# A two-layer hybrid block on one core: the second token tile's closing-norm steps and the next low parts queued behind the first tile's norm, two transfers issued from GpSimd's queue, and the last rows of the down weights split apart

## The chip, the cores and the metric

The kernel runs on one core of a Trainium2 chip. The metric is the device time of one execution in microseconds, the median of the runs; lower is better. The engines are named as the profile names them: PE (TensorE matmuls), PEld (its weight loads), DVE (VectorE), ACT (ScalarE), POOL (GpSimd) and SP (SyncE, which only issues transfers here). A name with a q (ACTq, SPq, POOLq) is that engine's instruction queue while it issues or waits.

## What is computed

Two layers act on 256 tokens of 1024 channels, all in float32. Each layer has a first feed-forward block, a mixer (convolution, recurrence and pooling side by side), cross-attention to a memory of 256 rows, and a second feed-forward block. Each of the four parts is closed by a layer norm of the residual sum. The change touches the feed-forward blocks and the norms that close them:

```python
def swiglu(x, w_gate, w_up, w_down):
    return (jax.nn.silu(x @ w_gate) * (x @ w_up)) @ w_down
...
for l in range(DEPTH):
    h = layer_norm(ALPHA * h + 0.5 * swiglu(h, ffn1_gate[l], ffn1_up[l], ffn1_down[l]), ln_g[l, 0], ln_b[l, 0])
    ...
    h = layer_norm(ALPHA * h + 0.5 * swiglu(h, ffn2_gate[l], ffn2_up[l], ffn2_down[l]), ln_g[l, 3], ln_b[l, 3])
return h
```

The line left out holds the mixer and the cross-attention, each with a layer norm of its own. The hidden width of the feed-forward blocks is 2816: five chunks of 512 columns and a last one of 256.

## The kernel before, in words

**Numbers in two parts.** PE multiplies a rounded form of float32. So every operand is split (`split`, L74 to L76): ACT casts it to the rounded form, the high part (`whi`, `ah`, `xTh`), and DVE subtracts that from the original and leaves the low part (`wlo`, `al`, `xTl`). A product is three matmuls into one sum: high by high, high by low, low by high (`mm_rows`, L153). Every weight passes through this: `load` (L78) issues the transfers of a slab of weights from SP into buffers called `raw` (six of 128 x 1024), and splits each buffer into a `whi` and a `wlo` (eight of each). A `raw` buffer is free for the next transfer once DVE has made its low part.

**Token tiles.** The 256 tokens are two tiles of 128, kept as `h[0]` and `h[1]` (`h0`, `h1` in the rows below). PE needs each of them transposed before the next block (`transposed`, L201: eight PE transposes, L196, whose results ACT and DVE split into `xT`).

**A feed-forward block** (`ffn`, L420) goes through the chunks. For each it makes the gate and up products, silu and their product, moves the result across partitions by four transfers (`turn`, L464, into a tile called `dealt`) and DVE transposes (L477), splits it into `ah` and `al`, and multiplies it by rows of the down weights into four sums `dn` (two tiles by two halves of the columns). In three of the four blocks the last chunk, 256 wide, goes through `by_seven` (L609): seven products of blocks in place of eight. There the gated product is made in the tile `both` (L723), two of its four transfers are issued by SP and two by ACT (L468, L469), and `slab(4, 0)`, `slab(4, 1)` and `slab(5, 0)` (L759) bring the last down weights. The products with these three slabs stand in the closing norm's function, by `tail` and `ending` (L846 to L862): all of tile 0 first, then tile 1's first half, then a part of its second half, then the transposes of `h[0]`, and the rest of tile 1.

**The closing norm** (`finish`, L323) does for tile 0 and then for tile 1: the residual sum of each half with its row sums (L352), the mean (L362), the sum of squares (L365, on ACT), the variance (L366), one over its root (L370, on POOL), subtraction of the mean and the gain (L373, two halves), scale and shift (L378, two halves). In the last norm of the program the statistics are made another way (L358, L368), and tile 1's second half is closed by two quarters (L339, L346).

**What sets the order.** Every engine runs its own instructions strictly in the order of its queue. That order is made by a scheduler when the program is built. `tc.issue_after(x)` is a hint to it: an instruction in that block which runs on the same engine as `x` is queued behind `x`. It puts nothing on the chip but the order. The norm of the first feed-forward block of layer 1 is followed by `keys` (L868), columns of `ca_k` by the memory `mT`; the norm of layer 0's second block is followed by the gate and up products of layer 1's first block (`first`, L494, the branch with `pend`), in which the transposes of `h[1]` (`pend`) stand in the middle of tile 0's up products.

Of the kernel before, what the change touches and what calls it, by code (L numbers as in the profile page):

```python
# [60 lines left out]
def model(ctx: ExitStack, tc: tile.TileContext, t: dict, out: bass.AP):  # L61
# [9 lines left out]

    loads, normed, lows, turns = [], [], [], []

    def split(hi, lo, src):  # L74
        nc.scalar.copy(hi, src)  # L75
        lows.append(nc.vector.tensor_tensor(lo, src, hi.bitcast(F32), op=ALU.subtract))  # L76

    def load(src, k0, nk, c0, ncol, fine=False, dealt=False, across=False):  # L78


        hi, lo, todo = [], [], []
        step = 2048 // ncol
        for a in range(k0, k0 + nk, step):
            half = step // 2
# [20 lines left out]
            for s in range(2):  # L105
                h = wp.tile([P, 1024], F32R, tag="whi", name="whi", bufs=8)
                w = wp.tile([P, 1024], F32R, tag="wlo", name="wlo", bufs=8)
                h = h.rearrange("p (k c) -> p k c", c=ncol)
                w = w.rearrange("p (k c) -> p k c", c=ncol)
                r = raw[s]  # L110
                if fine:
                    todo += [(h[:, b, :], w[:, b, :], r[:, b, :]) for b in range(half)]
                else:
                    split(h, w, r)
                hi.append(h)
                lo.append(w)
# [9 lines left out]
    def product(o, w, x, start, stop, more=False):  # L126
        x = x.rearrange("p (h c) -> p c h" if len(x.shape) == 2 else "p r (h c) -> p r c h", h=2)
        o = o.rearrange("p (c h) -> p c h" if len(o.shape) == 2 else "p r (c h) -> p r c h", h=2)
        nc.tensor.matmul(o, w, x, start=start, stop=stop, skip_group_check=more)  # L129

# [191 lines left out]

    def finish(mm, y, scale, gb, units, last=False, junk=None):  # L323

# [4 lines left out]
        g, b = gb  # L329
        for i in range(NT):  # L330

            st = sm.tile([P, 4, 6], F32, tag="st", name="st")
            pieces, size = [slice(0, 512), slice(512, DM)], 512
            if last and i == NT - 1:

                pieces, size = [slice(0, 512), slice(512, 768), slice(768, DM)], 256
                c = slice(512, DM)
                v = halves(h[i][:, c])
                nc.vector.scalar_tensor_tensor(v, v, ALPHA / scale, sums(y[i][1]), op0=ALU.mult, op1=ALU.add)  # L339
            for c in pieces:  # L340
# [36 lines left out]
            for c in pieces:  # L377
                normed.append(nc.vector.scalar_tensor_tensor(  # L378
                    h[i][:, c], h[i][:, c], rs, b[:, c], op0=ALU.mult, op1=ALU.add
                ))  # L380
                if last:
                    e = nc.scalar if c.start == 512 else nc.sync
                    e.dma_start(out[0, tok(i), c], h[i][:, c])
        return lambda keep=None: transposed(h[1], 1, xTh, xTl, units[1], keep)

# [34 lines left out]
    def ffn(l, name, n, pend=None, last=False, early=None):  # L420
        gate, up, down = (t[f"{name}_{x}"][l] for x in ("gate", "up", "down"))
        with tc.tile_pool(name="ffn", bufs=2, reuse_waits="tile") as fp:
# [41 lines left out]
            def turn(s):  # L464
                n = s.shape[2] // P
                x = fp.tile([P, 4, NT, P], F32, tag="dealt", name="dealt", bufs=1)[:, :, :, 0 : 32 * n]
                for a in range(4):
                    queue = nc.scalar if n < 4 and a % 2 else nc.sync  # L468
                    last_deal = queue.dma_start(x[a * 32 : a * 32 + 32], s[:, :, a * 32 * n : (a + 1) * 32 * n])  # L469

                deals.append(last_deal)

                def rest(behind=None):
                    ah, al = act_tiles()
                    d = fp.tile([P, NT, 4, P], F32, tag="up", name="square", bufs=1)[:, :, 0:n, :]
                    for i in range(NT):
                        nc.vector.transpose(  # L477
                            d[:, i].rearrange("p k (b r) -> p b k r", b=4),
                            x[:, :, i, :].rearrange("p b (k j) -> p b k j", k=n),
                        )  # L480
                    d = d.rearrange("p i k t -> p k i t")

                    def parts():
                        split(*(y[:, 0:n].rearrange("p k (i t) -> p k i t", i=NT) for y in (ah, al)), d)

                    if behind is None:
                        parts()
                    else:
                        behind.append(parts)
# [4 lines left out]
            def first():  # L494
# [70 lines left out]
                else:  # L565
                    for i in range(NT):
# [5 lines left out]
                        for k in range(NK):  # L572
                            if i == 0 and k == NK // 2:
                                pend(q[0:2])
                            products(ou, wu, i, k)
# [182 lines left out]

            def slab(c, u):  # L759
                w = load(down, c * 4 + 2 * u, 2, 0, DM, dealt=c < len(chunks) - 1)  # L760
                ah, al = acts[c]
                return w, ah[:, 2 * u : 2 * u + 2, :], al[:, 2 * u : 2 * u + 2, :]


            sevens = (2, 4) if early is not None else (2, 4, 5)
            passed, deals, turn_memory = [], [], None
            bx = []
# [68 lines left out]
            with ExitStack() as behind:  # L836
                if 5 in sevens:
                    behind.enter_context(tc.issue_after(deals[-1].ins))
                    behind.enter_context(tc.issue_after(passed[-1][1].ins))
                end = [slab(4, 0), slab(4, 1)]  # L840
                if 5 in sevens:
                    behind.enter_context(tc.issue_after(lows[-1].ins))
                    acts[5] = acts[5]()
                end.append(slab(5, 0))

# [17 lines left out]

            return finish(tail, ys, 0.5, gb, (idn, jdn) if name == "ffn1" else (pdn, pdn), last, None if last else squares)

# [517 lines left out]
```

## Time and profile before

| | us |
|---|---|
| median of three runs | 1073.31 (1070.99 to 1074.92) |
| the profiled execution, its own time | 1073.36 |
| its span, first to last instruction | 1071.4 |
| PE, DVE, ACT busy within the span | 1055.8, 933.4, 662.8 |

The page of the profile gives each engine's busy time as a share of the span. Matmuls overlap, so a busy PE is not PE at its full pace; the places at which PE waits are found in the view of waits and in the rows of the timeline. A row of the timeline holds the start and the length of an instruction (or of a run of equal ones, with their count), the engine, the line, what it writes and reads, and in square brackets the idle time of the engine before it with what ended it. A row of the chain of waits holds start, length and what.

### The profile page before, as it was taken

How to read it: one execution, taken by the hardware profiler on the slowest of the kernel's cores; microseconds unless marked ns; L12 is line 12 of the kernel's file. 1: busy time of each engine (PE TensorE's matmuls, PEld its weight loads, DVE VectorE, ACT ScalarE, POOL GpSimd, SP SyncE). 2: the span in 40 equal slices, each digit the busy share in tenths (PEclk: the TensorE clock that was granted, in tenths of full speed). 3: DMA queues.
4: the chain of work that ended last, by engine and by line, in shares of the span. 5: the costliest groups of instructions: out<-in, count | busy, mean ns of one | idle time of the engine just before them, and what ended most of it. 6: DMA issues, size and time to landing. Idle time of an engine off the chain costs nothing.

```text
span 1071.4 us, 16492 instructions
## 1 busy us (share of the span) xinstructions
PE 1055.8 (99%) x6014; PEld 936.4 (87%) x6014; DVE 933.4 (87%) x1246; ACT 662.8 (62%) x909; POOL 91.2 (9%) x122
## 2 busy tenths in 40 slices
PE   9999999999999999999999999999999999999996
PEld 7888888889899888889788888888898998888895
DVE  6999898989988789888898987879899788899787
ACT  6665775676557466665665655566764665675652
POOL 8001001000000001010001011010000000000000
PEclk9999999999999999999999999999999999999999
DMA  9999985754675589988788988867646765799971
GB/s 355 298 314 274 261 271 157 255 167 149 216 275 181 169 275 242 351 191 218 241 294 228 327 246 214 255 208 233 198 115 214 246 234 172 240 299 295 240 196 58
DMA packets 143745, 251.06 MB, mean 234 GB/s; under 512 B 12784, under 2 KB 53520, under 8 KB 143664
## 3 DMA queue, kind: packets, MB, share of 16 engines
q1 hardware_dynamic: 130656, 228.89, 64.6%
q0 software_dynamic: 10800, 19.55, 10.8%
q10 hardware_dynamic: 2208, 1.57, 0.5%
q8 instruction: 47, 0.77, 0.3%
q14 instruction: 34, 0.28, 0.1%
HBM read 234.50 MB, written 1.05 MB: 220 GB/s over the span
## 4 chain that ended last, share of the span: by engine, by line
PE 86%; DVE 5%; issue 3%; DMA 3%; ACT 1%; POOL 0%; ACTq 0%; DVEq 0%; SPq 0%; POOLq 0%
PE acc L129 58%; PE dn L129 25%; DVE wlo L76 2%; DMA raw<-in_ffn_gate_dram 2%; PE acc L196 1%; ACT whi L75 1%; DVE raw L646 1%; DMA raw<-in_w_out_dram 0%; PE dn L1068 0%; DMA h<-in_x_dram 0%; PE dn L1142 0%; PE acc L526 0%; DMA dealt<-both 0%; DVE h L378 0%; DVE yr L1221 0%
## 5 line engine op out<-in xcount | busy, mean ns | idle before, releaser
L76 DVE TENSOR_TENSOR wlo<-raw,whi 128x1024 fp32r<-128x1024 f32 (+1 forms) x453 | 535.9, 1212 | 55.0 <-ACT whi L75 50.3
L75 ACT CAST whi<-raw 128x1024 fp32r<-128x1024 f32 (+1 forms) x453 | 456.4, 1043 | 200.8 <-PE dn L129 58.2
L129 PE MATMUL acc<-whi,xT 128*128 128x512 f32 (+1 forms) x1064 | 313.8, 373 | 0.0
L129 PEld LDWEIGHTS acc<-whi,xT 128*128 128x128 f32 x1064 | 199.3, 189 | 26.5
L129 PE MATMUL acc<-wlo,xT 128*128 128x512 f32 (+1 forms) x532 | 197.9, 372 | 0.0
L129 PE MATMUL dn<-wlo,ah 128*128 128x512 f32 x346 | 131.7, 382 | 1.0 <-DVE wlo L76 1.0
L129 PE MATMUL dn<-whi,al 128*128 128x512 f32 x346 | 130.9, 381 | 0.0
L129 PE MATMUL dn<-whi,ah 128*128 128x512 f32 x346 | 130.7, 383 | 0.1
L129 PE MATMUL acc<-xT,whi 128*128 128x512 f32 x480 | 117.7, 382 | 0.1
L129 PEld LDWEIGHTS acc<-wlo,xT 128*128 128x128 f32 x532 | 100.7, 189 | 13.3
L129 PEld LDWEIGHTS acc<-xT,whi 128*128 128x128 f32 x480 | 86.8, 190 | 10.1 <-ACT whi L75 0.4
L129 PE MATMUL dn<-whi,xT 128*128 128x512 f32 x288 | 87.7, 381 | 0.0
L129 PEld LDWEIGHTS dn<-wlo,ah 128*128 128x128 f32 x346 | 65.9, 190 | 11.3 <-DVE wlo L76 2.2
L129 PEld LDWEIGHTS dn<-whi,ah 128*128 128x128 f32 x346 | 65.8, 190 | 9.8 <-ACT ah L75 0.8
L129 PEld LDWEIGHTS dn<-whi,al 128*128 128x128 f32 x346 | 65.9, 190 | 9.7 <-DVE al L76 0.4
L129 PEld LDWEIGHTS acc<-xT,wlo 128*128 128x128 f32 x480 | 62.9, 191 | 3.2
L129 PE MATMUL acc<-xT,wlo 128*128 128x256 f32 x480 | 63.3, 275 | 0.0
L129 PE MATMUL acc<-whi,kTl 128*128 128x512 f32 (+1 forms) x176 | 61.7, 351 | 0.0
L129 PE MATMUL acc<-wlo,kTh 128*128 128x512 f32 (+1 forms) x176 | 61.7, 351 | 0.0
L129 PE MATMUL acc<-whi,kTh 128*128 128x512 f32 (+1 forms) x176 | 61.7, 351 | 0.0
L129 PEld LDWEIGHTS dn<-whi,xT 128*128 128x128 f32 x288 | 54.4, 189 | 7.3
L129 PE MATMUL dn<-wlo,xT 128*128 128x512 f32 x144 | 54.8, 380 | 0.2 <-DVE wlo L76 0.2
(245 smaller groups left out, 1293.0 us busy)
## 6 DMA issues: line engine op xcount, KB each, us to landing
raw<-in_ffn_up_dram SPq DMA_DIRECT2D x88, 512.0 KB, 5.5
raw<-in_ffn_down_dram SPq DMA_DIRECT2D x88, 512.0 KB, 6.0
raw<-in_ffn_gate_dram SPq DMA_DIRECT2D x84, 512.0 KB, 5.6
raw<-in_w_in_dram SPq DMA_DIRECT2D x48, 512.0 KB, 4.7
dealt<-sg SPq DMA_DIRECT2D x80, 128.0 KB, 4.9
raw<-in_ffn_up_dram POOLq DMA_DIRECT2D x19, 512.0 KB, 6.3
raw<-in_ffn_gate_dram POOLq DMA_DIRECT2D x16, 512.0 KB, 9.9
raw<-in_ca_k_dram SPq DMA_DIRECT2D x16, 512.0 KB, 5.1
```

What stands on the lines that cost most here:

```text
L75: nc.scalar.copy(hi, src)
L76: lows.append(nc.vector.tensor_tensor(lo, src, hi.bitcast(F32), op=ALU.subtract))
L129: nc.tensor.matmul(o, w, x, start=start, stop=stop, skip_group_check=more)
L196: turns.append(nc.tensor.transpose(pt[:, k, :], src[:, (4 * j + k) * P : (4 * j + k + 1) * P], unit))
L646: nc.vector.tensor_tensor(r[i], r[i], plus[i], op=ALU.add)
```

## The change

It has seven parts. (1) In `finish`, tile 1's steps on DVE are queued behind the last step of tile 0's norm, in the norms after a block whose last chunk went through `by_seven`, except the program's last; there, the splits of the next `load` are queued behind the same step on DVE too (`guard`). (2) In the program's last norm the residual sum of tile 1's second half (L339) is queued behind the last low part. (3) Two of the four transfers of the last chunk's product are issued by POOL in place of ACT. (4) The loads of the last slabs are no longer queued behind the last of these transfers; since that one stood in ACT's queue, the casts of these slabs were what it held back. (5) `slab(5, 0)` is loaded with `fine`, so that its two buffers are split apart: the split of the last activations (`ah`, `al`) now stands between the two. (6) The DVE transposes of the last activations are made ahead of that slab's splits. (7) Matmuls of `product` now also count for the hints that name the last PE instruction, so that `pend` is queued behind the products written before it.

```diff
-        nc.scalar.copy(hi, src)
+        rounded = nc.scalar.copy(hi, src)
         lows.append(nc.vector.tensor_tensor(lo, src, hi.bitcast(F32), op=ALU.subtract))
+        return rounded
...
+        first = guard.pop() if guard else None
...
-                    split(h, w, r)
+                    with tc.issue_after(first) if first else nullcontext():
+                        split(h, w, r)
...
-        nc.tensor.matmul(o, w, x, start=start, stop=stop, skip_group_check=more)
+        turns.append(nc.tensor.matmul(o, w, x, start=start, stop=stop, skip_group_check=more))
...
-    def finish(mm, y, scale, gb, units, last=False, junk=None):
+    def finish(mm, y, scale, gb, units, last=False, junk=None, ordered=False):
...
-        for i in range(NT):
+        def tile_done(i):
...
-                nc.vector.scalar_tensor_tensor(v, v, ALPHA / scale, sums(y[i][1]), op0=ALU.mult, op1=ALU.add)
+                with tc.issue_after(lows[-1].ins):
+                    nc.vector.scalar_tensor_tensor(v, v, ALPHA / scale, sums(y[i][1]), op0=ALU.mult, op1=ALU.add)
...
+        tile_done(0)
+        with tc.issue_after(normed[-1].ins) if ordered else nullcontext():
+            if ordered:
+                guard.append(normed[-1].ins)
+            tile_done(1)
...
-                    queue = nc.scalar if n < 4 and a % 2 else nc.sync
-                    last_deal = queue.dma_start(x[a * 32 : a * 32 + 32], s[:, :, a * 32 * n : (a + 1) * 32 * n])
-
-                deals.append(last_deal)
+                    queue = nc.gpsimd if n < 4 and a % 2 else nc.sync
+                    queue.dma_start(x[a * 32 : a * 32 + 32], s[:, :, a * 32 * n : (a + 1) * 32 * n])
...
-                        nc.vector.transpose(
+                        dealt = nc.vector.transpose(
...
+                    dealts.append(dealt)
...
-                                pend(q[0:2])
+                                with tc.issue_after(turns[-1].ins):
+                                    pend(q[0:2])
...
-            def slab(c, u):
-                w = load(down, c * 4 + 2 * u, 2, 0, DM, dealt=c < len(chunks) - 1)
+            def slab(c, u, fine=False):
+                w = load(down, c * 4 + 2 * u, 2, 0, DM, fine, dealt=c < len(chunks) - 1)
...
                 if 5 in sevens:
-                    behind.enter_context(tc.issue_after(deals[-1].ins))
                     behind.enter_context(tc.issue_after(passed[-1][1].ins))
                 end = [slab(4, 0), slab(4, 1)]
                 if 5 in sevens:
                     behind.enter_context(tc.issue_after(lows[-1].ins))
-                    acts[5] = acts[5]()
-                end.append(slab(5, 0))
+                    acts[5] = acts[5](held)
+                    behind.enter_context(tc.issue_after(dealts[-1].ins))
+                end.append(slab(5, 0, 5 in sevens))
+                if 5 in sevens:
+                    rounded = split(*end[2][0].todo[0])
+                    with tc.issue_after(rounded.ins):
+                        held[1]()
+                    split(*end[2][0].todo[1])
...
-            return finish(tail, ys, 0.5, gb, (idn, jdn) if name == "ffn1" else (pdn, pdn), last, None if last else squares)
+            return finish(tail, ys, 0.5, gb, (idn, jdn) if name == "ffn1" else (pdn, pdn), last, None if last else squares, 5 in sevens and not last)
```

The rows that follow stand in the engines' queues; the line numbers are each kernel's own, and those of the changed one are 1 to 10 higher (L352, L366, L378 became L356, L370, L382). They come from the end of layer 0's second block.

On ACT, around the last chunk's product: `both` is that product's tile, `raw_5196`, `raw_5197`, `raw_5208` and `raw_5209` the buffers of `slab(4, 0)` and `slab(4, 1)`. Before:

```order
L678 COPY both_4969<-acc_4970 128x256
L454 ACTIVATE both_4969<-acc_4970 128x256
L75 CAST ah_5145<-square_5147 128x1024
L469 DMA dealt_5153<-both_4969 32x8x64 x2
L75 CAST whi_5200<-raw_5196 128x1024
L75 CAST whi_5204<-raw_5197 128x1024
L75 CAST whi_5212<-raw_5208 128x1024
L75 CAST whi_5216<-raw_5209 128x1024
```

and now:

```order
L688 COPY both_4969<-acc_4970 128x256
L75 CAST whi_5200<-raw_5196 128x1024
L75 CAST whi_5204<-raw_5197 128x1024
L75 CAST whi_5212<-raw_5208 128x1024
L464 ACTIVATE both_4969<-acc_4970 128x256
L75 CAST ah_5145<-square_5147 128x1024
L75 CAST whi_5216<-raw_5209 128x1024
L75 CAST whi_5229<-raw_5225 128x1024
```

Three casts moved ahead of the silu (L454, now L464), and the two transfers left the queue; they stand in POOL's now, ahead of the two steps L370 of this norm.

On DVE, the first tile's norm at the same end: `wlo_5363` to `wlo_5379` are low parts of the next block's gate weights. Before:

```order
L76 TENSOR_TENSOR wlo_5363<-raw_5358,whi_5362 128x1024
L352 SCALAR_TENSOR_TENSOR h0_72,st_5239<-h0_72,dn_4028 128x512
L352 SCALAR_TENSOR_TENSOR h0_72,st_5239<-h0_72,dn_4029 128x512
L76 TENSOR_TENSOR wlo_5367<-raw_5359,whi_5366 128x1024
L362 TENSOR_SCALAR mv_5278<-st_5239 128x1
L352 SCALAR_TENSOR_TENSOR h1_73,st_5288<-h1_73,dn_4030 128x512
L366 TENSOR_SCALAR rs_5279<-mv_5278 128x1
L373 SCALAR_TENSOR_TENSOR h0_72<-h0_72,mv_5278,lng_5141 128x512 x2
L378 SCALAR_TENSOR_TENSOR h0_72<-h0_72,rs_5279,lnb_5142 128x512 x2
L76 TENSOR_TENSOR wlo_5375<-raw_5370,whi_5374 128x1024
```

and now:

```order
L356 SCALAR_TENSOR_TENSOR h0_72,st_5239<-h0_72,dn_4028 128x512
L356 SCALAR_TENSOR_TENSOR h0_72,st_5239<-h0_72,dn_4029 128x512
L366 TENSOR_SCALAR mv_5278<-st_5239 128x1
L370 TENSOR_SCALAR rs_5279<-mv_5278 128x1
L377 SCALAR_TENSOR_TENSOR h0_72<-h0_72,mv_5278,lng_5141 128x512 x2
L382 SCALAR_TENSOR_TENSOR h0_72<-h0_72,rs_5279,lnb_5142 128x512 x2
L356 SCALAR_TENSOR_TENSOR h1_73,st_5288<-h1_73,dn_4030 128x512
L76 TENSOR_TENSOR wlo_5363<-raw_5358,whi_5362 128x1024
L76 TENSOR_TENSOR wlo_5367<-raw_5359,whi_5366 128x1024
```

Two low parts and one step of tile 1 moved from the front and the middle of tile 0's norm to behind it.

On DVE, a little later, the second tile's norm: `wlo_5387` to `wlo_5403` are the four low parts of the next block's up weights. Before:

```order
L76 TENSOR_TENSOR wlo_5379<-raw_5371,whi_5378 128x1024
L352 SCALAR_TENSOR_TENSOR h1_73,st_5288<-h1_73,dn_4031 128x512
L76 TENSOR_TENSOR wlo_5387<-raw_5382,whi_5386 128x1024
L362 TENSOR_SCALAR mv_5341<-st_5288 128x1
L76 TENSOR_TENSOR wlo_5391<-raw_5383,whi_5390 128x1024
L76 TENSOR_TENSOR wlo_5399<-raw_5394,whi_5398 128x1024
L366 TENSOR_SCALAR rs_5342<-mv_5341 128x1
L373 SCALAR_TENSOR_TENSOR h1_73<-h1_73,mv_5341,lng_5141 128x512 x2
L378 SCALAR_TENSOR_TENSOR h1_73<-h1_73,rs_5342,lnb_5142 128x512 x2
L76 TENSOR_TENSOR wlo_5403<-raw_5395,whi_5402 128x1024
```

and now:

```order
L356 SCALAR_TENSOR_TENSOR h1_73,st_5288<-h1_73,dn_4031 128x512
L76 TENSOR_TENSOR wlo_5375<-raw_5370,whi_5374 128x1024
L366 TENSOR_SCALAR mv_5341<-st_5288 128x1
L76 TENSOR_TENSOR wlo_5379<-raw_5371,whi_5378 128x1024
L76 TENSOR_TENSOR wlo_5387<-raw_5382,whi_5386 128x1024
L370 TENSOR_SCALAR rs_5342<-mv_5341 128x1
L377 SCALAR_TENSOR_TENSOR h1_73<-h1_73,mv_5341,lng_5141 128x512 x2
L382 SCALAR_TENSOR_TENSOR h1_73<-h1_73,rs_5342,lnb_5142 128x512 x2
L76 TENSOR_TENSOR wlo_5391<-raw_5383,whi_5390 128x1024
L76 TENSOR_TENSOR wlo_5399<-raw_5394,whi_5398 128x1024
L76 TENSOR_TENSOR wlo_5403<-raw_5395,whi_5402 128x1024
```

Of the up weights' low parts three stood ahead of tile 1's norm; one does now, and the other three stand behind it.

More of the change, by code (lines that the diff above doesn't have):

```diff
@@ L69, in acc @@
         return ps.tile(list(shape), F32, tag=tag, name=tag)
-    loads, normed, lows, turns = [], [], [], []
+    loads, normed, lows, turns, guard = [], [], [], [], []
     def split(hi, lo, src):
-        nc.scalar.copy(hi, src)
+        rounded = nc.scalar.copy(hi, src)
         lows.append(nc.vector.tensor_tensor(lo, src, hi.bitcast(F32), op=ALU.subtract))
+        return rounded
     def load(src, k0, nk, c0, ncol, fine=False, dealt=False, across=False):
@@ L765, in ffn @@
             sevens = (2, 4) if early is not None else (2, 4, 5)
-            passed, deals, turn_memory = [], [], None
+            passed, dealts, turn_memory = [], [], None
             bx = []
```

## The prediction

> **What bounds the kernel now.** I read the engines' busy time first, then PE's waits, then the timeline around each wait.
>
> ```profile
> span 1071.4 us, 16492 instructions
> ...
> PE 1055.8 (99%) x6014; PEld 936.4 (87%) x6014; DVE 933.4 (87%) x1246; ACT 662.8 (62%) x909; POOL 91.2 (9%) x122
> ...
> PE acc L196 <- DVE h L378: 3.7, 2, 1.9
> ...
> PE dn L129 <- DVE wlo L76: 1.3, 2, 1.0
> ```
>
> PE is busy 99% of the span, so no edit to the other engines can win more than PE's gaps. The waits that this change aims at are few: twice PE's transposes wait for tile 0's last norm step, 3.7 us together, and PE's down products wait 1.3 us for low parts. These places are the ends of three feed-forward blocks: at 531 us (layer 0's second; "first place"), 700 us (layer 1's first; "second") and 1048 us (the last; "third").
>
> ```profile
> 531.63 1.29 PE L196 MATMUL acc<-pdn,h 128*128 128x128 f32 x8 [1.85 <-DVE h L378]
> ...
> 700.70 1.29 PE L196 MATMUL acc<-idn,h 128*128 128x128 f32 x8 [1.85 <-DVE h L378]
> ...
> 702.00:706.00 4.00, 4.00 (x12) 3.20 (x12) 2.69 (x4) 2.98 (x4) 0.00 (x0) 0.59 0.51 141
> ...
> 1048.40 0.48 PE L129 MATMUL dn<-wlo,ah 128*128 128x512 f32 x1 [1.05 <-DVE wlo L76]
> ```
>
> Each norm costs PE 1.85 us. Behind the second one PE's granted clock is 0.59 from 702 to 706 us: 4 x 0.41 = 1.6 us more. Behind the first there is no such stretch, so one such gap in two was followed by it.
>
> **First place, what goes.** DVE's and ACT's rows there:
>
> ```profile
> 525.71 0.69 DVE L352 SCALAR_TENSOR_TENSOR h<-h,dn 128x512 f32<-128x512 f32 x1
> ...
> 526.32 1.22 DVE L76 TENSOR_TENSOR wlo<-raw,whi 128x1024 fp32r<-128x1024 f32 x1
> 527.46 0.21 DVE L362 TENSOR_SCALAR mv<-st 128x1 f32<-128x1 f32 x1
> 528.74 0.69 DVE L352 SCALAR_TENSOR_TENSOR h<-h,dn 128x512 f32<-128x512 f32 x1 [1.06 <-PE dn L129]
> ...
> 529.35 0.15 DVE L366 TENSOR_SCALAR rs<-mv 128x1 f32<-128x1 f32 x1
> 529.41 1.40 DVE L373 SCALAR_TENSOR_TENSOR h<-h,mv,lng 128x512 f32<-128x512 f32 x2
> 530.74 1.41 DVE L378 SCALAR_TENSOR_TENSOR h<-h,rs,lnb 128x512 f32<-128x512 f32 x2
> 533.20 1.28 DVE L76 TENSOR_TENSOR xT<-acc,xT 128x512 fp32r<-128x512 f32 x2
> ...
> 537.42 2.35 DVE L76 TENSOR_TENSOR wlo<-raw,whi 128x1024 fp32r<-128x1024 f32 x2
> ...
> 527.71 1.15 ACT L365 ACTIVATE kTh<-h,mv 128x1024 fp32r<-128x1024 f32 x1 [3.94 <-DVE mv L362]
> 528.76 0.18 ACT L365 ACTIVATION_READ_ACCUMULATOR kTh<-h,mv 128x1 f32 x1
> ```
>
> DVE starts its next instruction about 0.08 us before the end of the last, so a low part takes 1.14 us of its queue (526.32 to 527.46), a residual sum 0.61, a norm half 0.66, two `xT` halves 1.20. From the start of tile 0's second sum (525.71) to its first finished half (530.74 + 0.75) are 5.8 us. The low part in between goes (1.14), and so does tile 1's sum in front of L366, which then starts when the square is read out (528.94) and not at 529.35: 0.4. That leaves 4.2 us. PE's own work ahead of the transposes ends where it did, at 529.8 (531.63 - 1.85), so the sum must start by 525.6; its start comes next.
>
> ```profile
> 512.21 0.68 DVE L723 TENSOR_TENSOR both<-both 128x512 f32<-128x512 f32 x1
> ...
> 515.62 4.63 DVE L76 TENSOR_TENSOR wlo<-raw,whi 128x1024 fp32r<-128x1024 f32 x4 [1.59 <-ACT whi L75]
> 520.17 0.77 DVE L477 STREAM_TRANSPOSE square<-dealt 128x256 f32<-128x256 f32 x2
> ...
> 511.12 0.38 ACT L454 ACTIVATE both<-acc 128x256 f32<-128x256 f32 x1 [2.04 <-PE acc L129]
> ...
> 512.92 1.57 ACTq L469 DMA_DIRECT2D dealt<-both  x2
> 514.54 5.78 ACT L75 CAST whi<-raw 128x1024 fp32r<-128x1024 f32 x6 [2.10 <-DVE al L76]
> ...
> dealt<-both ACTq DMA_DIRECT2D x6, 64.0 KB, 5.0
> wpool<-in_pool_w_dram POOLq DMA_DIRECT2D x2, 64.0 KB, 5.8
> ...
> L211 POOL DMA_DIRECT2D early<-in_mem_dram x4: 587/602/657, 102.2 to 104.0; - x4
> ...
> DMA to landing us min/median/max: 5.2/5.7/7.7
> ```
>
> ACT was held 2.10 us by issuing the two transfers, and DVE then idled 1.59 us. Now three casts of 0.96 us (5.78 / 6) run in ACT's 2.04 us ahead of silu, which comes 0.9 us later, at 512.0, and is done by 512.4; DVE is busy until 512.2 anyway, so the product ends at 513.0 and not at 512.9. Behind it stand five subtractions of 1.14 us without the 1.59 us gap, and the transposes of the dealt tile could start at 518.7 where they started at 520.17. Their data must be there. What POOL needs for two such transfers the trace doesn't show. **From below** it is ACT's 5.0 us for the same 64 KB; **from above** the 7.7 us of the slowest of its transfers from memory with 0.6 us each to issue. I take the row of the same size, 5.8 us. The second lands at 513.0 + 0.6 + 5.8 = 519.4: 0.7 us late for DVE, still 0.8 us earlier than before. Tile 0's second sum then starts about 525.2 (PE is what it waits for), its norm's first half is done at 529.4, and PE's transposes start with PE's own queue, at about 530.0: **1.6 us won**.
>
> **First place, what comes.** PE's next needs, from the chain of waits:
>
> ```profile
> 532.92 2.59 PE dn L129 x12
> 535.51 7.77 PE acc L129 x36
> 543.28 0.87 PE acc L196 x8
> ...
> raw<-in_ffn_up_dram SPq DMA_DIRECT2D x88, 512.0 KB, 5.5
> ```
>
> One product takes 0.216 us (7.77 / 36). After the transposes (0.87) and 12 down products (2.59) come 24 gate products, and the eighth up product needs the second low part of up: 0.87 + 2.59 + 31 x 0.216 = 10.2 us, so at 540.2. In DVE's queue that low part now stands behind tile 1's whole norm. DVE: first half done 529.4, second 530.1; residual sum 0.61, two lows 2.28, `xT` 1.20, residual sum 0.61, low 1.14, mean 0.13, two lows 2.28: 538.4. Now L366 waits for ACT's square, and ACT has a cast of the third up buffer ahead of it. That buffer's transfer is issued once the first gate low, now behind the norm, frees a `raw`: 530.1 + 0.61 + 1.22 = 531.9; it lands 5.5 us later, at 537.4, the cast ends at 538.4, the square with its read-out at 539.7. Then 0.07 + 1.32 + 1.33 for the norm and 1.22 for the low: 543.6. **PE waits 3.4 us** where it had none: net 1.8 us lost here. A gap nearly twice 1.85 us is likelier than not to be followed by the half clock, 1.6 us; I count it.
>
> By the Trainium skill, "TensorE: Matmul & The Clock Gate", Part 1: The HAM clock gate, the clock halves only after an idle window of about 3.4 us; by that rule neither old gap could do it, the trace disagrees with its 1.85 us, and the sum without this term would be 1073.9. The skill's "DMA: Bandwidth & Descriptors", Specifications, gives about 1 us to the first byte from GpSimd and 0.6 from the others; by it a transfer takes 5.4 us, the second lands 0.4 us earlier, and the sum would fall by at most 0.8 us over the places where it is late.
>
> **Second place.** The old gap (1.85) and its slow stretch (1.6) go. Here `keys` follows.
>
> ```profile
> 706.27 7.86 PE acc L129 x48
> ...
> 706.31 0.69 DVE L352 SCALAR_TENSOR_TENSOR h<-h,dn 128x512 f32<-128x512 f32 x1 [1.62 <-PE dn L129]
> ...
> 708.88 0.15 DVE L366 TENSOR_SCALAR rs<-mv 128x1 f32<-128x1 f32 x1 [1.62 <-ACT kTh L365]
> ```
>
> PE needs tile 1's first half 0.87 + 2.59 + 7.86 = 11.3 us after tile 0's transposes begin. DVE's queue is the one above: 0.66 + 0.61 + 1.22 to the first low, 5.5 for the transfer behind it, 1.0 and 1.3 on ACT, 0.07 + 1.32 + 0.75: 12.4 us. That is 1.1 us of wait, and the low parts of `w_in` come behind it: seven DVE pieces of 7 us against 5 us of PE work, 2.0 more. Net -3.5 + 3.1 = **-0.4 us**; the 1.62 us gaps that DVE had here are the slack that could make it less.
>
> **Third place.**
>
> ```profile
> 1046.53 0.69 DVE L339 SCALAR_TENSOR_TENSOR h<-h,dn 128x512 f32<-128x512 f32 x1 [2.60 <-PE dn L129]
> ```
>
> L339 stood in DVE's queue ahead of all low parts and waited 2.60 us for PE, which then waited 1.05 us for them. Behind the last low it costs nothing: 1.05 us and some 0.15 of smaller waits go. The second POOL transfer may land late again, 0.3: **-0.9 us**. No norm of a second tile with lows behind it follows.
>
> **At nothing** I cost the order of matmuls within the last slabs (same matmuls; the lows for them come earlier than before), the same for eight matmuls in layer 1's keys, and 58 rows of SP's queue in layer 1's first block (PE waits for no transfer there in its waits; if that cover went, one 512 KB transfer, 5.5 us). POOL's next instruction behind the transfers, the norm's root, comes 10 us later.
>
> **Sum.** First place +1.8 and the half clock +1.6, second -0.4, third -0.9: +2.1. The profiled execution's own time is 1073.36 us, its span and 2 us around it, as good as the median 1073.31. Forecast: 1075.5 us.
>
> **Rivals.** (a) POOL's transfers land late, **slower**. Each microsecond over 5.8 stops DVE and then PE at all three places: 3 us. From 6.9 us on the kernel is over 0.5% (5.4 us) slower, which is about what a measurement can tell from no change; at 7.7 it is 1081.2. For it: POOL's slowest row, and 512 KB loads in flight beside it. Against: its 64 KB row. Chance 0.26. (b) The wait moves only in part: the up buffer lands early enough not to hold ACT (wait 2.1 and not 3.4), no half clock, 2.0 and not 3.1 at the second place: -1.6 + 2.1 - 3.5 + 2.0 - 1.2 = -2.2, 1071.2. Chance 0.25. (c) All the old gaps go and nothing comes, **faster**: -1.6 - 3.5 - 1.2 = -6.3, 1067.1. It needs 3.4 us of DVE time after 530 us, and DVE's timeline marks no idle time there from 529.35 to 544. Chance 0.05. The forecast's own case, 1073 to 1078, has 0.44. Faster 0.05, within 0.5% 0.69, slower 0.26. The range takes (b) and most of (a): 1070 to 1080.5.
>
> **What would show it.** Right: no wait of L196 on L378 left, a wait of an `acc` product on a `wlo` of about 3 us near 541, L339 without a wait, `dealt<-both` on POOL at about 5.8 us. Wrong: that wait missing (the second step fails), or transposes L477 far behind the five subtractions (the transfers).

## The result, and the profile after

The changed kernel takes **1067.28 us** (median of 7 runs, 1066.09 to 1069.4); the kernel before took 1071.5 us beside it (7 runs, 1069.65 to 1074.92). The ratio is 0.9959, its 95% interval 0.9941 to 0.9977: faster by 0.41%, within the half per cent that the prediction called the limit of what can be told, but clearly a gain and not the 2.1 us of loss that the sum gave; the forecast was 1075.5 us, and its range began at 1070. The profiled execution took 1069.4 us, the slowest of the seven (before: 1073.36), and the reading below is made on these two.

First the page of the changed kernel, its span and busy times, then its view of PE's waits (total, times, longest):

```profile
span 1067.7 us, 16492 instructions
...
PE 1054.8 (99%) x6014; PEld 937.0 (88%) x6014; DVE 933.8 (87%) x1246; ACT 661.6 (62%) x909; POOL 94.6 (9%) x128
```

```profile
PE acc L132 <- DVE wlo L76: 2.6, 3, 1.9
PE dn L516 <- DVE kTh L511: 1.5, 1, 1.5
PE acc L535 <- DMA h<-in_x_dram: 0.4, 1, 0.4
```

The two waits of PE's transposes on the norm (3.7 us) are gone, and so is the wait of the down products on low parts (1.3). What has come is a wait of `acc` products on low parts: 2.6 us, 1.9 of it in one piece. So the wait did move to where the prediction put it; but it is smaller than what was removed.

Now PE's timeline of the changed kernel: the start of the transposes of `h[0]` at the first place, the new wait there, the same transposes at the second place, and the two small new waits behind them.

```profile
528.21 1.04 PE L199 MATMUL acc<-pdn,h 128*128 128x128 f32 x8
...
540.39 0.69 PE L132 MATMUL acc<-wlo,xT 128*128 128x512 f32 x1 [1.87 <-DVE wlo L76]
...
698.91 0.93 PE L199 MATMUL acc<-idn,h 128*128 128x128 f32 x7
...
704.86 0.49 PE L132 MATMUL acc<-mT,wlo 128*128 128x256 f32 x2 [0.36 <-DVE wlo L76]
717.10 0.49 PE L132 MATMUL acc<-xT,wlo 128*128 128x256 f32 x2 [0.40 <-DVE wlo L76]
```

The transposes stood at 531.63 and 700.70 before: PE is 3.42 us ahead at the first place, but only 1.79 at the second, so between the two it gives back 3.5 us and gains the old gap of the second place (1.85). The 3.5 us are the wait of 1.87 and what stands in the windows view of the changed kernel (the number behind the five engines' busy times is PE's granted clock):

```profile
536.00:540.00 4.00, 2.53 (x12) 1.88 (x10) 4.00 (x7) 1.55 (x2) 0.92 (x1) 1.00 0.97 353
540.00:544.00 4.00, 3.61 (x12) 3.05 (x13) 3.21 (x4) 0.32 (x1) 0.00 (x0) 0.57 1.04 369
...
702.00:706.00 4.00, 3.64 (x20) 3.13 (x19) 4.00 (x7) 2.68 (x4) 0.16 (x2) 1.00 0.77 257
```

Behind the wait the clock is 0.57 for 4 us: 4 x 0.43 = 1.7 us. At 702 us, where the kernel before stood at 0.59, it is whole now. By place, counting PE's matmuls through in both traces (changed minus before; "predicted" is the prediction's own sum):

| | predicted, us | measured, us |
|---|---|---|
| start of the kernel (its first wait, for a transfer of `x`, is 0.4 us and was 1.1) | 0 | -0.8 |
| first place | +3.4 | +1.0 |
| second place | -0.4 | -2.6 |
| third place | -0.9 | -1.6 |
| the rest, and around the span | 0 | 0.0 |
| sum | +2.1 | -4.0 |

The 0.8 us at the start are not the change's: in the ten traces of the experiments the first wait is 0.3 to 0.6 us, so the 1.1 belongs to that one execution of the kernel before.

### The profile page after: what moved, and what is told of

Read it like the earlier page. It is cut to its first block, busy times and chain, and to the rows that moved or that the text cites. A ratio compares the mean times of both kernels' runs of the same rounds, so it can differ in the third digit from the quotient of the medians.

```text
span 1067.7 us, 16492 instructions
## 1 busy us (share of the span) xinstructions
PE 1054.8 (99%) x6014; PEld 937.0 (88%) x6014; DVE 933.8 (87%) x1246; ACT 661.6 (62%) x909; POOL 94.6 (9%) x128
## 3 DMA queue, kind: packets, MB, share of 16 engines
HBM read 234.50 MB, written 1.05 MB: 221 GB/s over the span
## 4 chain that ended last, share of the span: by engine, by line
PE 91%; DVE 5%; DMA 2%; issue 1%; ACT 1%; DVEq 0%; POOL 0%; ACTq 0%; SPq 0%
PE acc L132 60%; PE dn L132 28%; DVE wlo L76 2%; PE acc L199 1%; ACT whi L75 1%; PE dn L1083 0%; DMA raw<-in_w_out_dram 0%; DMA dealt<-both 0%; DVE h L382 0%; DMA raw<-in_w_in_dram 0%; PE dn L1157 0%; DMA raw<-in_ffn_down_dram 0%; DVE raw L656 0%; DMA h<-in_x_dram 0%; DVE xT L76 0%
```

## The experiments

Two theories were put against each other. **A**: part (1), the queue order behind tile 0's norm, wins the norm's gap and pays part of it back on the low parts. **B**: what wins the gap is that ACT's casts no longer wait behind the two transfers (parts 3 and 4), so DVE reaches the norm earlier whatever the order; part (1) only moves low parts to where PE waits for them. All times are medians beside runs of the kernel before on the same chip (1071.0 to 1071.6 us).

| run | what it is | us | ratio to before, 95% |
|---|---|---|---|
| e1 | changed, without part 1 | 1064.38 | 0.9937 [0.9925, 0.9948] |
| e2 | before, with part 1 alone | 1069.60 | 0.9982 [0.9973, 0.9991] |
| e3 | changed, transfers on ACT | 1067.21 | 0.9967 [0.9955, 0.9978] |
| e4 | changed, without part 2 | 1067.62 | 0.9968 [0.9956, 0.9979] |
| e5 | e1 without parts 5 and 6 | 1064.44 | 0.9940 [0.9927, 0.9953] |
| e6 | e1 without parts 3 and 4 | 1067.44 | 0.9968 [0.9956, 0.9980] |
| e7 | changed, up's low part ahead of tile 1's norm | 1064.90 | 0.9946 [0.9934, 0.9958] |
| e8 | e1 with six more DVE instructions in tile 0's norm at the first two places | 1074.91 | 1.0037 [1.0023, 1.0052] |
| e9 | before, with part 4 alone | 1063.71 | 0.9929 [0.9916, 0.9942] |
| e10 | before, with part 2 alone | 1069.69 | 0.9986 [0.9976, 0.9996] |

**e1, part 1 taken back.**

```diff
-                guard.append(normed[-1].ins)
+                pass
```

This frees the low parts. Tile 1's steps keep their hint; e9, which lacks it, has tile 1's first sum at the same place in DVE's queue, behind tile 0's norm.

> The changed kernel with part (1) taken back: the next load's low parts are free again to stand ahead of tile 0's norm (on every engine this gives the same order as taking all of part (1) back). Now two of them stand ahead of tile 0's residual sums at the first and second place. Theory A (part 1 wins the norm's gap): the two subtractions of 1.14 us push the norm back and PE waits for L382 again, 1.85 us at each place with half clock behind one of them: about 1071. Theory B (what freed DVE is the casts that ACT no longer holds back; part 1 only moves low parts behind the norm): DVE idles 1.04 and 0.60 us ahead of the two sums in the changed kernel, the two low parts (2.28 us) fill that and push the norm back by about 0.5 us, which is less than the 0.6 us by which L382's first half was ready ahead of PE's transposes; the wait of 1.93 us on up's second low part goes, and the half clock behind it where it occurs: 1063.5 to 1065.5.

1064.38 us, and its slowest run (1065.14) is faster than the fastest of the changed kernel (1066.09): theory B, at the price it named. Its view of PE's waits has nothing left at the first two places:

```profile
PE dn L516 <- DVE kTh L511: 1.5, 1, 1.5
PE acc L535 <- DMA h<-in_x_dram: 0.5, 1, 0.5
PE dn L132 <- DVE wlo L76: 0.2, 1, 0.2
```

Why the low parts cost nothing ahead of the norm is read off DVE's timeline. In the changed kernel DVE has run out of work when it comes to tile 0's residual sums (L356):

```profile
517.29 0.76 DVE L485 STREAM_TRANSPOSE square<-dealt 128x256 f32<-128x256 f32 x2
...
521.93 0.69 DVE L356 SCALAR_TENSOR_TENSOR h<-h,dn 128x512 f32<-128x512 f32 x1 [1.04 <-PE dn L132]
...
523.23 0.69 DVE L356 SCALAR_TENSOR_TENSOR h<-h,dn 128x512 f32<-128x512 f32 x1 [0.60 <-PE dn L132]
...
526.88 1.41 DVE L382 SCALAR_TENSOR_TENSOR h<-h,rs,lnb 128x512 f32<-128x512 f32 x2
```

In e1 the low parts that part (1) forbids there fill that time (three stand in a row ahead of the sums, two of them the next load's):

```profile
519.02 3.49 DVE L76 TENSOR_TENSOR wlo<-raw,whi 128x1024 fp32r<-128x1024 f32 x3
522.43 0.68 DVE L356 SCALAR_TENSOR_TENSOR h<-h,dn 128x512 f32<-128x512 f32 x1
...
523.03 0.68 DVE L356 SCALAR_TENSOR_TENSOR h<-h,dn 128x512 f32<-128x512 f32 x1
...
526.67 1.41 DVE L382 SCALAR_TENSOR_TENSOR h<-h,rs,lnb 128x512 f32<-128x512 f32 x2
```

The norm ends at the same place in time in both, and PE's transposes start at 527.57 here. The 1.64 us (1.04 + 0.60) in which the changed kernel's DVE idles ahead of the sums are about the time that it lacks at 540 us, where PE waits 1.87.

**e2, part 1 alone.** The diff is the part's own, on the kernel before:

```diff
+        tile_done(0)
+        with tc.issue_after(normed[-1].ins) if ordered else nullcontext():
+            if ordered:
+                guard.append(normed[-1].ins)
+            tile_done(1)
...
+                    with tc.issue_after(first) if first else nullcontext():
+                        split(h, w, r)
```

> The kernel before with part (1) alone. Theory A: both norm gaps (1.85 us each) and the half clock behind the second go, a wait on up's second low part of about 2 us comes with half clock behind it: 1071.5 - 3.7 - 1.6 + 2 + 1.7 = about 1069.9, and down to 1068 without the half clock; L339 still waits. Theory B: DVE is late by 1.6 us (ACT held by the issue of the two transfers), so the low parts behind tile 1's norm come later than in the changed kernel and PE's wait on them is 3 us or more: 1070.5 to 1072, no gain.

1069.60 us, a gain of 1.7 and nearest to A's figure; B's "no gain" is wrong. PE's timeline shows the two norm gaps down from 1.85 to 0.23 and 0.22:

```profile
528.41 1.29 PE L198 MATMUL acc<-pdn,h 128*128 128x128 f32 x8 [0.23 <-DVE h L380]
...
539.33 1.29 PE L198 MATMUL acc<-pdn,h 128*128 128x128 f32 x8 [0.35 <-DVE h L380]
...
604.05 0.48 PE L131 MATMUL acc<-whi,xT 128*128 128x512 f32 x1 [2.34 <-ACT halves L686]
...
699.58 1.29 PE L198 MATMUL acc<-idn,h 128*128 128x128 f32 x8 [0.22 <-DVE h L380]
```

So part (1) does close the gap when nothing else does. Both theories expected a wait of 2 us or more on up's second low part as well, and both are wrong there: this run has none. The second row shows why. The transposes of `h[1]` stand behind 31 gate and up products here and behind 36 in every other trace, so PE makes them while it would have waited, and it comes to the product that needs the low part at 540.95, when the low part is just done (540.9). This run lacks part (7), which queues these transposes behind all products written before them. So the price of part (1) at the first place, 1.87 us, is paid in an order in which PE does not make the transposes first. That part (7) is what forbids it is argued from what this part does: the change without part (7) was not run.

The third row is a wait that no other kernel shows: at 604 us ACT stood 2.8 us without a gate load. Its runs scatter from 1067.06 to 1071.26 us at one and the same clock (0.998 and 0.999), so that wait may differ from run to run; why this order makes it was not settled.

**e3, the transfers on ACT again.**

```diff
-                    queue = nc.gpsimd if n < 4 and a % 2 else nc.sync
+                    queue = nc.scalar if n < 4 and a % 2 else nc.sync
```

> The changed kernel with part (3) taken back: the two transfers of the last chunk's product are issued by ACT again; the order of all other instructions is the same. Theory A: PE does not notice it, 1067.3 (within 0.5). Theory B (ACT's queue is what matters): ACT is held about 2.1 us behind the product at all three places and the casts behind it come late; DVE idles 1.6 us there, its slack ahead of the residual sums (1.0 us) takes most of it and the rest, 0.5 to 1.5 us, comes out at PE at each place: 1068.5 to 1071.

1067.21 against 1067.28: which queue issues the transfers is worth nothing here, against B's figure for it. It is not the issue of the two transfers that costs, but what stands behind it in ACT's queue.

**e4, part 2 taken back.**

```diff
-                with tc.issue_after(lows[-1].ins):
+                if True:
                     nc.vector.scalar_tensor_tensor(v, v, ALPHA / scale, sums(y[i][1]), op0=ALU.mult, op1=ALU.add)
```

> The changed kernel with part (2) taken back: in the last norm L343 stands in DVE's queue ahead of the dealt tile's transposes and the last low parts and waits there for PE. If part (2) carries the third place, PE waits about 1.5 us for the low parts that come late: 1068.5 to 1070. If the earlier low parts of parts (3) to (6) already cover the wait, 1067.3.

1067.62, at most 0.4 us more than the changed kernel and e3: the earlier low parts cover the wait. On DVE's timeline of this run L343 stands ahead of the dealt tile's transposes and no longer waits:

```profile
1040.90 3.49 DVE L76 TENSOR_TENSOR wlo<-raw,whi 128x1024 fp32r<-128x1024 f32 x3
1044.30 0.68 DVE L343 SCALAR_TENSOR_TENSOR h<-h,dn 128x512 f32<-128x512 f32 x1
1044.90 0.76 DVE L485 STREAM_TRANSPOSE square<-dealt 128x256 f32<-128x256 f32 x2
```

**e5 and e6, which part of the rest.** e5 takes parts (5) and (6) off e1, e6 takes (3) and (4) off it:

```diff
-                    acts[5] = acts[5](held)
-                    behind.enter_context(tc.issue_after(dealts[-1].ins))
-                end.append(slab(5, 0, 5 in sevens))
...
+                    acts[5] = acts[5]()
+                end.append(slab(5, 0))
```

> The kernel of e1 (the changed kernel without part 1, 1064.4) with parts (5) and (6) taken back as well: the last down slab is split in one piece, and its first low part stands ahead of the dealt tile's transposes again. Theory B1 (the casts freed by part 4 alone carry the gain): DVE's queue holds the same instructions ahead of tile 0's sums, only in another order, so 1064.4 within 0.7. Theory B2 (parts 5 and 6 carry it): the last `al` comes 1.2 us later, PE waits for it or the norm comes later at each of the three places: 1066 to 1068.

```diff
-                    queue = nc.gpsimd if n < 4 and a % 2 else nc.sync
-                    queue.dma_start(
+                    queue = nc.scalar if n < 4 and a % 2 else nc.sync
+                    last_deal = queue.dma_start(
...
+                    behind.enter_context(tc.issue_after(deals[-1].ins))
```

> The kernel of e1 with parts (3) and (4) taken back: ACT issues the two transfers, and the casts of the last slabs stand behind them again. Theory B1: DVE idles about 1.6 us behind the product as in the kernel before, tile 0's sums start 1.6 to 2.7 us later than in e1, where the norm was ready only 0.15 us ahead of PE's transposes; so PE's wait on L382 comes back with 1.5 to 2 us at both places, with half clock behind one of them, and 0.5 us or more at the third: 1068.5 to 1071. Theory B2: 1064.4 to 1065.5.

e5 is e1 (1064.44): parts (5) and (6) are worth nothing. e6 is 1067.44, 3.1 us slower: B1's mechanism, a microsecond below its range. The gaps come back, but shorter, as PE's timeline of e6 shows:

```profile
529.73 1.29 PE L199 MATMUL acc<-pdn,h 128*128 128x128 f32 x8 [1.49 <-DVE h L382]
...
698.46 1.29 PE L199 MATMUL acc<-idn,h 128*128 128x128 f32 x8 [1.49 <-DVE h L382]
```

2 x 1.49 = 3.0 us are the 3.1, and no half clock stood behind them.

**e7, the wait on up's low part removed.** Part (1) is kept, but at the first place the steps of tile 1's norm from L370 on are written behind the second low part of up:

```diff
+            if norm and held_norm:
+                with tc.issue_after(lows[-1].ins):
+                    held_norm.pop()()
+                first = normed[-1].ins
```

> The changed kernel, part (1) kept, but at the first place tile 1's norm (from L370 on) stands behind up's second low part in place of ahead of it. PE needed that low part at 538.46 and tile 1's first normed half 1.1 us later. Theory (the wait on the low part is the cost of part 1 there): the low part is done at about 537.6, tile 1's first half at 539.7, so the wait falls from 1.93 to 0.2 us: 1065.5, and the half clock that follows it in some runs goes too. Rival (DVE is simply behind by that much work, and the wait moves to tile 1's transposes): 1067.3.

1064.90: 2.4 us less than the changed kernel. The wait of 1.87 is gone, and what is left of it at tile 1's transposes is small:

```profile
539.00 1.29 PE L203 MATMUL acc<-pdn,h 128*128 128x128 f32 x8 [0.22 <-DVE h L389]
```

So that one wait, with the half clock that sometimes follows, was most of the price of part (1) (2.4 of the 2.9 us between the changed kernel and e1), and DVE was not behind by the whole of it.

**e8, a longer gap.**

```diff
+            if ordered and i == 0:
+                for d in range(6):
+                    nc.vector.bn_stats(st[:, 2 + d % 2, :], h[i][:, 0:512])
```

> The kernel of e1 with six more statistic instructions of about 0.61 us each (results not read) ahead of tile 0's mean at the first and second place. In e1 the norm was ready 0.15 us ahead of PE at the first place and 0.1 us behind it at the second. If DVE's queue ahead of the norm is paid one to one there, PE waits about 3.5 us for L382 at each place (3.7 at the second): 1064.4 + 7.2 = 1071.6 if the clock stays whole. Gaps of 1.85 to 1.93 us were followed by half clock in two of five profiled cases, one of 2.3 us was not. If the chance grows with the gap, 1.7 us more behind one or both: 1073.3 to 1075. If DVE has slack that I do not see: under 1069.

1074.91, with the half clock. The gaps in the profiled run are the foretold size, and the clock falls behind both (PE's timeline, then windows):

```profile
532.17 1.94 PE L199 MATMUL acc<-pdn,h 128*128 128x128 f32 x8 [3.46 <-DVE h L385]
...
705.24 1.94 PE L199 MATMUL acc<-idn,h 128*128 128x128 f32 x8 [3.65 <-DVE h L385]
```

```profile
530.00:534.00 4.00, 1.83 (x9) 1.86 (x10) 3.38 (x8) 2.32 (x3) 0.93 (x1) 0.60 0.00 0
534.00:538.00 4.00, 4.00 (x12) 3.22 (x12) 3.57 (x4) 2.76 (x4) 0.00 (x0) 0.55 0.14 14
...
702.00:706.00 4.00, 0.76 (x4) 0.80 (x5) 3.05 (x6) 2.80 (x4) 1.84 (x2) 0.86 0.02 7
706.00:710.00 4.00, 4.00 (x18) 3.51 (x17) 3.22 (x6) 2.66 (x4) 0.00 (x0) 0.72 0.00 0
```

1064.4 + 7.1 of gaps is 1071.5; the other 3.4 us of the median go with the half clock. In the profiled run (1075.6 us) the clock is at half for 6.83 us from 530.77 and for 3.41 us from 704.85. Of these, 1.40 and 0.39 us lie within the gaps, where PE loses nothing: (6.83 + 3.41 - 1.40 - 0.39) / 2 = 4.2 us, and 1071.5 + 4.2 is 1075.7. DVE's queue ahead of the norm is paid one to one: there is no slack left in e1.

**e9 and e10, one part alone on the kernel before.** e9 takes out one line:

```diff
-                    behind.enter_context(tc.issue_after(deals[-1].ins))
```

> The kernel before with one line taken out: the casts of the last slabs are no longer queued behind the two transfers on ACT (part 4 alone; ACT still issues the transfers). If the freed casts alone carry the gain, both norm gaps go and nothing takes their place, and the third place keeps up to 0.8 us of its wait, since L339 still stands ahead of the low parts: 1064.5 to 1066. If it needs another part beside it (the transfers on POOL, or L339 moved): 1067 to 1069.5, about what e6 (1067.4) gives from the other side.

e10 puts the order of part (2) in:

```diff
+                with tc.issue_after(lows[-1].ins):
+                    nc.vector.scalar_tensor_tensor(v, v, ALPHA / scale, sums(y[i][1]), op0=ALU.mult, op1=ALU.add)
```

> The kernel before with part (2) alone: L339 behind the last low part of the last norm; nothing else moves on any engine. By the prediction's third term PE's wait of 1.05 us and 0.15 of smaller waits go: 1071.2 - 1.2 = 1070.0. If DVE is late there for another reason (its 1.6 us wait for the held casts), under 0.5 us is won: 1070.8 or more.

e9 takes 1063.71 us, **7.9 us less than the kernel before beside it (1071.64) and 3.6 less than the whole change** (3.2 by the ratios); it can't be told from e1 (the intervals overlap), but it is one line. In the kernel before, ACT waited 2.04 us ahead of the silu (L454) and then 2.10 us at the two transfers, with casts queued behind both. On ACT's timeline of e9 three casts stand ahead of the silu, which has no gap any more:

```profile
506.91 2.94 ACT L75 CAST whi<-raw 128x1024 fp32r<-128x1024 f32 x3
509.75 0.38 ACT L454 ACTIVATE both<-acc 128x256 f32<-128x256 f32 x1
...
510.89 1.60 ACTq L469 DMA_DIRECT2D dealt<-both  x2
512.53 2.94 ACT L75 CAST whi<-raw 128x1024 fp32r<-128x1024 f32 x3 [1.46 <-DVE wlo L76]
```

ACT still issues the transfers and still stands 1.46 us there, but DVE has low parts to make meanwhile; its 1.59 us gap is gone, and with it PE's waits at all three places. e10 takes 1069.69, 2.0 us less by the medians and 1.5 by the ratio (0.4 to 2.6 by its interval), and the wait of 1.05 us is gone from its trace: the prediction's third term (1.2) holds when part (2) stands alone.

## Why the prediction was wrong, point by point

Between the sum of +2.1 us and the measured -4.0 lie 6.1: 2.4 at the first place, 2.2 at the second, 0.7 at the third, and the 0.8 at the start that the change did not make. The forecast missed by 2 us more because of its base: the three runs behind 1073.3 us lay high, and the median of seven is 1071.5.

**The mechanism at the first place was right, its size was not.** The old gap went and PE came to wait for the second low part of up behind tile 1's norm, as foretold; 3.4 us were predicted and 1.87 measured. The step that failed is the transfer behind the first gate low. "It lands 5.5 us later, at 537.4" was the median of 88 transfers; this one followed a low part that ended at 529.95, was issued at 530.10 and was there at 533.7, after 3.6 us, among the shortest of the 88 (3.6 to 10.5). It met idle DMA engines: their share is 0.00 from 527 to 530 us. DVE's and ACT's timelines of the changed kernel:

```profile
528.81 2.35 DVE L76 TENSOR_TENSOR wlo<-raw,whi 128x1024 fp32r<-128x1024 f32 x2
...
536.41 0.14 DVE L370 TENSOR_SCALAR rs<-mv 128x1 f32<-128x1 f32 x1
536.48 1.40 DVE L377 SCALAR_TENSOR_TENSOR h<-h,mv,lng 128x512 f32<-128x512 f32 x2
537.80 1.41 DVE L382 SCALAR_TENSOR_TENSOR h<-h,rs,lnb 128x512 f32<-128x512 f32 x2
539.12 3.49 DVE L76 TENSOR_TENSOR wlo<-raw,whi 128x1024 fp32r<-128x1024 f32 x3
```

```profile
533.80 1.06 ACT L75 CAST whi<-raw 128x1024 fp32r<-128x1024 f32 x1 [1.14 <-DMA raw<-in_ffn_up_dram]
534.76 1.15 ACT L369 ACTIVATE kTh<-h,mv 128x1024 fp32r<-128x1024 f32 x1
```

So the square ended at 536.0 and not at 539.7, L370 did not wait for it, and the low part began at 539.12. The sum also took too little for what goes: by the count of matmuls it was 2.8 us and not 1.6, since PE met no gap at all at the transposes and lost 0.6 us less on its way there, at 521 to 525 us. What came was 3.8 us, with the half clock, and not 5.0.

Rival (b), with a chance of 0.25, named this step: the up buffer lands early enough not to hold ACT, and the wait is 2.1 us. Its time of 1071.2 is still 4 us too long: for the base, for what goes, and because less came at the second place too.

**The half clock was counted as certain, and comes in some executions only.** Behind the 1.87 us wait it stood in the profiled run of the changed kernel (0.57) and not in e3's, which has the same wait to the hundredth:

```profile
540.13 0.48 PE L132 MATMUL acc<-wlo,xT 128*128 128x512 f32 x1 [1.87 <-DVE wlo L76]
```

```profile
540.00:544.00 4.00, 3.87 (x22) 3.48 (x23) 4.00 (x6) 1.50 (x3) 0.00 (x0) 1.00 1.03 382
```

Of the changed kernel's seven runs two have a clock of 0.996 (1069.4 and 1069.09 us) and five 0.998 or 0.999 (1066.09 to 1067.83). The prediction's forecast of 1075.5 holds 1.6 us for it that the median does not have. What decides it is in the last section.

**The gain was put down to the wrong part.** The prediction let the gap close because a low part (1.14) and tile 1's sum (0.4) left DVE's queue, and priced the freed casts as 1.6 us of slack that the low parts behind the norm did not see. e1 shows the reverse: with the casts freed the gaps stay closed without part (1), and part (1) then adds 2.9 us. e2 and e9 show that either closes them alone; together they win the gap only once. Rival (c), all old gaps gone and nothing in their place, was held at 0.05 because DVE has no idle time after 530 us. Its 1067.1 us lies next to the measured 1067.28 by luck: the new waits did come, and the kernel that has none, e1, takes 1064.4. That row was true and the conclusion was not: the idle time stood ahead of the norm, at 522 us, where the changed order lets no low part stand.

**Second place.** The old gap and its half clock went as predicted (3.9 us by the count of matmuls, 3.5 in the sum). Of 3.1 us of new waits 1.3 came (the rows of 0.36 on the keys' weights and 0.40 on `w_in`, and what the matmuls beside them lost). The transfer was early again; DVE's first low part there, and the cast that waited for the buffer behind it:

```profile
699.51 1.22 DVE L76 TENSOR_TENSOR wlo<-raw,whi 128x1024 fp32r<-128x1024 f32 x1
```

```profile
704.70 1.04 ACT L75 CAST whi<-raw 128x1024 fp32r<-128x1024 f32 x1 [1.32 <-DMA raw<-in_w_in_dram]
```

From 700.7 to 704.7 are 4.0 us, not 5.5 (the DMA share is 0.00 from 698 to 701 us here): that alone takes the 1.1 us that were predicted for tile 1's transposes, which do not wait.

**Third place.** -0.9 predicted, -1.6 measured. The cause given (L339 no longer blocks DVE) is one of two that each suffice: e10 shows it alone, e4 shows that the casts cover nearly all of it without it.

**POOL's transfers (rival a, slower).** 5.8 us was taken, with 7.7 as the upper bound; they take 4.1, and DVE's transposes of that tile (L485, at 517.29 in the timeline above) run without a wait. The rows of the DMA view:

```profile
dealt<-both SPq DMA_DIRECT2D x6, 64.0 KB, 4.1
dealt<-both POOLq DMA_DIRECT2D x6, 64.0 KB, 4.1
```

The Trainium skill, "DMA: Bandwidth & Descriptors", Specifications, gives about 1 us to the first byte from GpSimd and about 0.6 from the queues of SP and ACT, so a transfer of POOL would come 0.4 us later by an estimate. The trace does not show it: the four land alike at each place here (3.5 to 5.4 us from SP, 3.4 to 5.3 from POOL), and in 4.9 and 5.2 us by the median where SP and ACT issue them (e3).

## What to carry to other kernels

Before pricing an order that protects one instruction, look for idle time ahead of it: low parts that are forbidden to stand there are owed later, and here PE paid for them. What such a debt costs depends on whether the engine that waits has other work that it may take first. When several edits aim at one gap, each may close it alone; take them off one at a time, since the rest can cost (one deleted line beat the whole change by 3.6 us). A hint that queues cheap work behind an instruction that waits, such as a transfer on a compute engine's queue, stalls the engine that feeds on this work.

## What the runs showed of the hardware

**Whether the clock falls after a short gap depends on where the gap lies.** The kernel before has two gaps of 1.85 us, and its 45 runs beside e1, e5 and e9 fall into three groups by their mean granted clock:

| mean clock | runs | us |
|---|---|---|
| 0.998 to 0.999 | 12 | 1069.24 to 1070.36 |
| 0.996 to 0.997 | 22 | 1070.64 to 1071.89 |
| 0.995 | 11 | 1072.24 to 1072.96 |

The groups lie 1.4 to 1.6 us apart by their medians (1069.7, 1071.3, 1072.7), which is one stretch of half clock each: none, one or two of the two gaps. That makes (22 + 2 x 11) / 90 = 0.49 of the gaps. No run of e6, with two gaps of 1.49 us, is below 0.998 (six runs); of e8, with gaps of 3.5 us, all six are at 0.997 or below.

One of e1's five runs is at 0.997 too (1064.67 us), though e1's trace has no such gap; so the mean clock alone does not part the first two groups sharply.

What decides it can be read from the traces. A stretch of half clock behind a gap lasts 3.41 us (the kernel before, the changed kernel, e10, the second of e8) or twice that (the first of e8, 6.83). Another one starts at the end of every trace. Within a trace the starts lie whole multiples of 3.413 us apart: 107 times in the kernel before (701.87 and 1067.10 us), 153 in the changed kernel (540.54 and 1062.78), 156 in e10, 51 and 107 in e8. So there are windows of 3.413 us, and they begin at another place in each trace, 0.3 to 3.2 us behind the start of the span. The table counts PE's idle time by these windows (PE's ends are modelled by the profile).

| trace and place | gap, us | most idle time in one window, us | half clock behind it |
|---|---|---|---|
| before, first | 1.85 | 1.43 | no |
| before, second | 1.85 | 1.89 | from 701.87 |
| changed, first | 1.87 | 1.87 | from 540.54 |
| e10, first | 1.85 | 1.85 | from 531.53 |
| e10, second | 1.85 | 1.76 | no |
| e3, first | 1.87 | 1.31 | no |
| e4, first | 1.87 | 1.14 | no |
| e6, first and second | 1.49 | 1.09 and 1.52 | no |
| e2, at 604 us | 2.34 | 1.49 | no |
| e8, first | 3.46 | 2.06 | from 530.77 |
| e8, second | 3.65 | 3.27 | from 704.85 |

With 1.85 us or more in one window the clock fell at its end, five times of five; with 1.76 or less it did not. So a gap of 1.85 us has to lie almost whole within one window. An estimate from these figures: that is so for (3.41 - 1.85) / 3.41 = 0.46 of the places where it can begin, up to 0.51 if 1.76 us are enough, and 0.49 were counted. The wait of 2.34 us in e2 was shared by two windows, 1.49 and 0.85. That none of e2's 12 runs has a clock under 0.998 stays open: if each had this wait, about 0.6 of them should fall by the same estimate.

By the Trainium skill, "TensorE: Matmul & The Clock Gate", Part 1: The HAM clock gate, activity is judged in a window of about 3.4 us that runs free of the kernel. The traces agree with that window; but the page's limit for gaps, 3.4 us, is too high for this kernel, where 1.85 us were enough.
